# Conformer taps queued behind gate, low half and cast, and spread over the pointwise units

## The chip, the cores and the metric

The kernel runs on one core of one Trainium2 chip. The metric is the device time of one execution in microseconds (us). The engines are TensorE (PE; its weight loads are PEld), VectorE (DVE), ScalarE (ACT), GpSimd (POOL) and SyncE (SP); SP, ACT and POOL also issue DMAs. Each engine takes its instructions in the order of its own queue.

## The reference

A trunk of two layers over 512 positions and 1024 channels, in float32, with one final RMSNorm. The first layer mixes tokens with a gated DeltaNet, the second with the Conformer's convolution module; each then has cross-attention into 256 memory rows and a squared-ReLU MLP. The change is in the second layer's convolution module:

```python
def conformer_conv(h, w_pw1, b_pw1, w_dw, b_dw, ln_g, ln_b, w_pw2, b_pw2):
    u = h @ w_pw1 + b_pw1
    u = u[..., :D_MODEL] * jax.nn.sigmoid(u[..., D_MODEL:])
    c = causal_depthwise_conv(u, w_dw) + b_dw          # 31 taps per channel
    c = jax.nn.silu(layer_norm(c, ln_g, ln_b))
    return c @ w_pw2 + b_pw2
```

## The kernel before

Weights are kept at float32's accuracy by splitting: a half of a weight tile (128 rows, 1024 columns, 512 KB) is loaded by SP into `raw`, ScalarE casts it to the matmul type (`wh`, the high half, line 259), and VectorE or POOL subtracts that from the raw value (`wl`, the low half, line 73). TensorE then does three matmuls for each 128 columns: high by high, high by the low half of the activations, low by high. Three `wh`/`wl` pairs are held (`NW`), so a cast can write only when TensorE is done with the pair three units back. `wsplit` makes these pairs; `POOL_LO` lists the units whose low half POOL makes (7, 8, 10 to 16, 18 and 20 of the Conformer layer), all others are VectorE's.

The Conformer layer runs the units of `CONV_SEQ`: 16 pointwise units (24 matmuls each, two units to one of eight channel tiles `m`, in the order `MORD` = 0, 1, 4, 2, 5, 3, 6, 7), then 16 units of the next cross-attention's keys and values, which are there to keep TensorE busy. "Unit 13" below is the fourteenth of these 32. After each second pointwise unit `pw_ev` makes the gate of a channel tile: two products on VectorE (`sg`, `pa`), a sigmoid on ScalarE, and the gate itself on VectorE (line 79, writing `pa` or `gl`).

The 31-tap convolution is done in three ways. Tiles 4 to 7: the gate `gl` is stored to DRAM by ScalarE's queue, read back in another order into `xg` by SP's queue (`spill`, `fill`), and convolved by matmuls (`conv`, tile `cv`), after which VectorE adds the bias (`cyp`). Tiles 1, 2 and 3: one VectorE instruction for each tap (line 1547, "a tap", accumulating in PSUM in `ca`). Tile 0: a product on ScalarE (`cvp`, line 1530) and an addition on POOL (line 73) for each tap. The last five taps of tile 3 are also products and POOL's additions (`cb`), joined by one VectorE addition. When a tile's last tap is done, ScalarE copies the result out of `ca` (lines 1534, 1550, 1568), and four transposes (`cvT`, `turn`) bring it to rows of positions. LayerNorm's statistics are VectorE's (`bn`, line 1618); their sums over groups go through two tiny matmuls (`ln`, line 1654) whose operand is `lw`.

`TAPS_U` says how many taps of VectorE are put into the program after each unit, and `taps_pool(2)` puts two products and additions after each. A scheduler then orders each engine's queue; it may let an instruction pass earlier ones that are not ready by its own reckoning. `tc.issue_after(x)` keeps what is traced inside it behind `x` on `x`'s engine. Before the change only units from 16 on hold VectorE's taps back in this way (the list `gate`, from the unit before); `wsplit` also holds some casts and low halves back.

Of the kernel before, what the change touches and what calls it, by code (L numbers as in the profile page):

```python
# [11 lines left out]
ALU = mybir.AluOpType  # L12
# [26 lines left out]
def tile_trunk(ctx, tc, xT, memT, x_d, mem_d, prm_d, adt_d, bdw_d, tap_d, fin_d, first_d, w_ab, w_kq, w_v, w_z, w_dno, w_pw1, w_pw2,  # L39
# [14 lines left out]
    def nm(s):  # L54
        cnt[0] += 1
        return f"{s}_{cnt[0]}"

    def slot(dt=F32, s="u", shape=(P, NT)):
        return up.tile(list(shape), dt, tag="u", name=nm(s))
# [12 lines left out]
    def tt(e, o, a, b, op):  # L72
        r = e.tensor_tensor(out=o, in0=a, in1=b, op=op)  # L73
        if e is pool:
            last_pool[:] = [r]
        return r

    def stt(o, a, s, b, op0, op1):
        return dve.scalar_tensor_tensor(out=o, in0=a, scalar=s, in1=b, op0=op0, op1=op1)  # L79
# [17 lines left out]
    def pc(name, i=0):  # L97
        return (gn0 if name == "dn_norm" else prm)[:, OFF[name] + i:OFF[name] + i + 1]
# [128 lines left out]
    ws = {"next": 0, "split": 0, "load": 1, "raw": {0: raw0}, "hl": {}}  # L227
# [4 lines left out]
    def wload():  # L232
        u = ws["load"]
        ws["load"] += 1
        src = loads[u]
        raw = fsp.tile([P, 1024], F32, tag="fs", name=nm("t")) if u in sums7 else raw_tile()
        nc.sync.dma_start(out=raw, in_=src[0])
        for a in src[1:]:
            more(raw, a)
        ws["raw"][u] = raw  # L240
# [5 lines left out]
    def wsplit():  # L246
        u = ws["split"]
        ws["split"] += 1
        while ws["load"] <= need[u]:
            wload()  # L250
        (kind, i, *j), hf = order[u]
        raw = combos7(i, j[0], hf) if kind == "dn7" else ws["raw"].pop(need[u])
        h = wp.tile([P, 1024], F32R, tag="wh", name=nm("wh"), bufs=NW)
        lo = wp.tile([P, 1024], F32R, tag="wl", name=nm("wl"), bufs=NW)
        first = behind.get((kind, 0, 0) if kind == "pw2" else (kind, i, hf))
        if first is None and u in (3, 4):
            first = [ws["rb"]]
        with tc.issue_after(first[0].ins) if first else behind_merge():
            ins = [act.copy(h, raw)]  # L259
        if u < 3:  # L260
            tc.keep_in_program_order(ins[0])
        gp = u - conv0 in POOL_LO
        low = first[1] if first and len(first) > 1 else ws.get("tap")
        with tc.issue_after(low.ins) if low else nullcontext():
            ins.append(tt(pool if gp else dve, lo, raw, h.bitcast(F32), ALU.subtract))
        if not gp:
            ws["ins"] = ins[1]
        if u < 3:
            tc.keep_in_program_order(ins[1])
        ws["hl"][u] = (h, lo)  # L270
        if kind == "dn7":
            after7(i, j[0], hf)

    def wnext(key, hf):
        i = ws["next"]
        assert order[i] == (key, hf), (order[i], key, hf)
        while ws["load"] <= need[min(i + NRAW + 1 + 2 * (order[i][0][0] in ("up", "dn7")), len(order) - 1)]:
            wload()
        ready = NW - (order[i] == (("do", 1), 1) or i in (conv0 - 1, conv0)) if i > 2 else (1, 2, 1)[i]
        while ws["split"] < min(i + ready, len(order)):  # L280
            wsplit()
        ws["next"] += 1
        return ws["hl"].pop(i)
# [3 lines left out]
    def behind_merge():  # L287
        return tc.issue_after(ahead[0].ins) if ahead else nullcontext()
# [3 lines left out]
    def combos7(layer, g, u):  # L292
        name, h = order7(layer, g)[u // 2][1], u % 2
        if name == "T4" or name == "T2" and g < 3:
            return T7[h]
        t = ws["raw"].pop(need[u + base7[layer, g]])
        if name == ("T2" if g == 3 else "T1"):
            T7[h] = t
        return t

    def after7(layer, g, u):
        name, h = order7(layer, g)[u // 2][1], u % 2
        if name == "T2" or name == "T1" and g < 3:
            more(T7[h], block(layer, g, "22" if name == "T1" else "21", h))
# [119 lines left out]
    def root_table():  # L424
        tc.keep_in_program_order(act.activation(small(1), eps_ln, AF.Sqrt))
# [666 lines left out]
    def phased(t):  # L1092
        return t.rearrange("p (t s) -> p s t", s=PH)

    def by_phase(t):
        return t.rearrange("p (s t) -> p s t", s=PH)
# [368 lines left out]
    def conformer(norm, hres, nxt, rest):  # L1465
        xs = norm.xs
        st, x16 = {}, {}
# [8 lines left out]
        def pw_mm(i, hf):  # L1476
            m = MORD[i]
            w, st[m, hf] = wnext(("pw1", i), hf), psum("pw")
            if i:
                return proj(w, xs, st[m, hf], inside={STAT: lambda: (norm.stat(), pw_ev(0))} if (i, hf) == (1, 0) else None)  # L1480
            proj(w, xs, st[m, hf], 0, 4)
            if hf == 0:
                st["w"] = w
                return rest()
            proj(st.pop("w"), xs, st[0, 0], 4, 8)
            proj(w, xs, st[0, 1], 4, 8)

        def pw_ev(m):
            sg = slot(s="sg")
            tt(dve, sg, st.pop((m, 1)), norm.rb, ALU.mult)  # L1490
            act.activation(sg, sg, AF.Sigmoid, bias=pc("b_pw1", 8 + m))
            a = slot(s="pa")
            pa = tt(dve, a, st.pop((m, 0)), norm.rb, ALU.mult)
            if m < NTAP:
                x = wp.tile([P, 544], F32, tag="cv", name=nm("xn"), bufs=NCV)[:, 0:542]
                pool.memset(x[:, 0:30], 0.0)
                stt(a, a, pc("b_pw1", m), sg, ALU.add, ALU.mult)
                act.copy(phased(x[:, 30:542]), by_phase(a))
                (todo if m else todo_p).extend((dve_conv if m else pool_conv)(m, x))
                return  # L1500
            gl, x = [t.rearrange("p (j t) -> p j t", t=34) for t in (
                fsp.tile([P, 1024], F32, tag="fs", name=nm("gl"))[:, 0:544],
                wp.tile([P, 544], F32, tag="cv", name=nm("xg"), bufs=NCV))]
            with tc.issue_after(pa.ins):
                dve.memset(gl[:, :, 0:2], 0.0)
            stt(gl[:, :, 2:34], by_phase(a), pc("b_pw1", m), by_phase(sg), ALU.add, ALU.mult)
            x16[m] = x, gl, drp.tile([P, PH, 34], F32, tag="gd", name=nm("gd"))

        def spill(m):
# [8 lines left out]
        todo, todo_p, acc = [], [], {}  # L1518
# [52 lines left out]
            return [lambda d=d: tap(d) for d in range(n)] + [join]  # L1571

        def taps_pool(n):
            for _ in range(min(len(todo_p), n)):
                todo_p.pop(0)()

        def taps_dve(n):
            for _ in range(min(len(todo), n)):
                todo.pop(0)()
# [118 lines left out]
        gate, stack = [], ExitStack()  # L1698
        for i, (kind, u) in enumerate(CONV_SEQ):
            if kind == "p":  # L1700
                pw_mm(*divmod(u, 2))
                if u % 2 and u > 1:
                    pw_ev(MORD[u // 2])
            else:
                kv_unit(1, u, (LN_SUM[i], lnw.pop("sum")) if i in LN_SUM else None)

            for ins in gate:
                stack.enter_context(tc.issue_after(ins.ins))
            taps_dve(TAPS_U[i])
            stack.close()  # L1710
            taps_pool(2)
            for what, m, *more_ in after.pop(i, ()):
                {"t": taps, "c": conv, "l": ln, "s": lambda m: root_table(), "o": ln_out, "d": turn,
                 "m": moments, "w": spill, "r": fill}[what](m, *more_)
                if what == "c":
                    for ins in gate:
                        stack.enter_context(tc.issue_after(ins.ins))
                    taps_dve(TAPS_C[m])
                    stack.close()
                taps_pool(1 if what == "c" else 0)  # L1720
            gate = [x for x in (ws["ins"], mem.get("kf")) if x is not None] if i >= 15 else []
# [45 lines left out]
    nc.sync.dma_start(out=prm, in_=prm_d)  # L1767
    nc.sync.dma_start(out=adt, in_=adt_d.partition_broadcast(P))
    wsplit()
    for c in range(4):  # L1770
        if c == 3:
# [77 lines left out]
    for gq in range(2):  # L1849
# [12 lines left out]
        a, b = (4 * gq, 4 * gq + 1), (4 * gq + 2, 4 * gq + 3)  # L1862
# [7 lines left out]
        n = 0  # L1870
# [59 lines left out]
    h, rest = mlp7(0, n2, h, n3, lambda: (mem_gain(1, 0), taps(NTAP, *range(9)), selections()))  # L1930
    n4 = Norm("xa_norm1")
    h = conformer(n3, h, n4, rest)
    n5 = Norm("mlp_norm1")
    h = xattn(1, n4, h, n5)
# [45 lines left out]
TAPQ = {0: 12, 4: 44}  # L1980
TAPV = (37, 38, 39, 40, 69, 69, 70, 71)
STAT = 3
TAPS_U = (4,) * 7 + (6,) * 9 + (3,) * 8 + (0,) * 8
TAPS_C = {4: 0, 5: 0, 6: 0, 7: 0}
SHARE = 5
POOL_LO = (7, 8, 10, 11, 12, 13, 14, 15, 16, 18, 20)
# [113 lines left out]
```

## Time and profile before

| | |
|---|---|
| median of 3 runs | 1440.28 us (1439.27 to 1440.81) |
| the profiled execution | 1439.24 us, its span 1437.5 us |
| TensorE busy | 1426.3 us (99% of the span), granted clock 0.999 |
| VectorE, ScalarE, POOL busy | 1053.9, 760.8, 242.6 us |
| the Conformer layer | pointwise units about 787 to 887 us, keys and values to about 942 us of the span |
| in 785 to 890 us | TensorE 102.4, VectorE 93.6, ScalarE 60.6, POOL 66.2 of 105 us |

Busy time of TensorE is modelled, since its matmuls are pipelined: a step from one matmul of 512 columns to the next is 0.23 us, and the row shows 0.39. What counts is its idle time. Rows of a timeline give the start in us, the duration, the engine, the line, what is written and read, and in brackets how long the engine was idle before it and what ended that.

### The profile page before, as it was taken

What the parts mean: (1) busy time and instruction counts of PE and PEld (TensorE: products, weight loads), DVE (VectorE), ACT (ScalarE), POOL (GpSimd) and SP (SyncE); (2) the same over time, 40 slices, a digit from 0 to 9 for tenths busy, and PEclk for the clock granted to TensorE, in tenths of its full rate; (3) what the DMA queues carried; (4) which work ended last, traced back from release to release, by engine and by line L of the source; (5) the groups of instructions that cost most, each with busy time, mean ns of one, the idle gap of its engine ahead of it and who ended that gap; (6) DMA issues with size and microseconds to landing.
All of it is one profiled execution on the core that took longest, in us unless ns stands there. A gap on an engine that the chain in (4) does not pass through costs nothing.

```text
span 1437.5 us, 20460 instructions
## 1 busy us (share of the span) xinstructions
PE 1426.3 (99%) x7786; PEld 1191.4 (83%) x7786; DVE 1053.9 (73%) x1629; ACT 760.8 (53%) x1279; POOL 242.6 (17%) x244
## 2 busy tenths in 40 slices
PE   9999999999999999999999999999999999999998
PEld 7887888888888888888888878888888888888886
DVE  6989999877555766767679799985555766767677
ACT  6757856655444454434355655564444644444354
POOL 1302200102113010010000378111112010010100
PEclk9999999999999999999999999999999999999999
DMA  8232225522214576575766448742215476675853
GB/s 301 72 117 75 70 92 162 190 86 92 74 46 128 150 177 175 143 204 132 195 166 208 154 131 250 261 151 92 74 52 139 119 184 167 148 213 136 219 148 89
DMA packets 71859, 207.83 MB, mean 145 GB/s; under 512 B 15440, under 2 KB 16592, under 8 KB 71760
## 3 DMA queue, kind: packets, MB, share of 16 engines
q1 hardware_dynamic: 60960, 169.22, 36.1%
q0 software_dynamic: 9792, 35.66, 14.3%
q10 hardware_dynamic: 1008, 1.64, 0.3%
q8 instruction: 61, 1.00, 0.3%
q14 instruction: 38, 0.31, 0.1%
HBM read 203.28 MB, written 3.21 MB: 144 GB/s over the span
## 4 chain that ended last, share of the span: by engine, by line
PE 94%; DVE 3%; ACT 1%; issue 1%; POOL 1%; DMA 0%; SPq 0%; DVEq 0%; POOLq 0%; ACTq 0%
PE up L319 8%; PE up L320 8%; PE up L321 8%; PE dn L1263 7%; PE dn L1264 7%; PE dn L1265 7%; PE h L319 3%; PE h L320 3%; PE h L321 3%; PE xo L320 2%; PE q L320 2%; PE q L321 2%; PE xo L319 2%; PE xo L321 2%; PE q L319 2%; PE pw L319 2%
## 5 line engine op out<-in xcount | busy, mean ns | idle before, releaser
L259 ACT CAST wh<-raw 128x1024 fp32r<-128x1024 f32 x259 | 271.0, 1050 | 326.3 <-issue 98.1
L73 DVE TENSOR_TENSOR wl<-raw,wh 128x1024 fp32r<-128x1024 f32 (+1 forms) x251 | 307.8, 1228 | 92.0 <-ACT wh L259 89.9
L319 PE MATMUL up<-xh,wh 128*128 128x512 f32 x512 | 199.6, 390 | 0.0
L321 PE MATMUL up<-xh,wl 128*128 128x512 f32 x512 | 199.5, 390 | 0.0
L320 PE MATMUL up<-xl,wh 128*128 128x512 f32 x512 | 199.4, 390 | 0.0
L319 PEld LDWEIGHTS up<-xh,wh 128*128 128x128 f32 x512 | 96.1, 188 | 20.1
L321 PEld LDWEIGHTS up<-xh,wl 128*128 128x128 f32 x512 | 96.1, 188 | 19.9
L320 PEld LDWEIGHTS up<-xl,wh 128*128 128x128 f32 x512 | 96.2, 188 | 19.9
L244 POOL DMA_DIRECT2D t<-w_dn x48 | 42.1, 915 | 378.1 <-DVE wl L73 271.9
L1263 PE MATMUL dn<-wh,ah 128*128 128x512 f32 (+1 forms) x260 | 100.7, 387 | 0.0
L1265 PE MATMUL dn<-wl,ah 128*128 128x512 f32 (+1 forms) x260 | 100.6, 387 | 0.0
L1264 PE MATMUL dn<-wh,al 128*128 128x512 f32 (+1 forms) x260 | 100.5, 387 | 0.0
L79 DVE SCALAR_TENSOR_TENSOR rl<-up,rb 128x512 f32<-128x512 f32 x64 | 44.2, 690 | 58.7 <-PE up L321 58.7
L259 ACT CAST wh<-t 128x1024 fp32r<-128x1024 f32 x44 | 46.4, 1054 | 57.3 <-PE dn L1264 42.4
L73 DVE TENSOR_TENSOR wl<-t,wh 128x1024 fp32r<-128x1024 f32 x44 | 53.8, 1224 | 30.2 <-ACT wh L259 30.1
L73 POOL TENSOR_TENSOR sq<-sq,sq 128x512 f32<-128x512 f32 x26 | 42.8, 1648 | 168.4 <-ACT sq L447 151.3
L1547 DVE SCALAR_TENSOR_TENSOR ca<-xn,prm,ca 128x512 f32<-128x512 f32 x85 | 64.0, 753 | 5.2 <-ACT ca L1544 2.9
L73 DVE TENSOR_TENSOR acc<-acc,dn 128x512 f32<-128x512 f32 x99 | 66.6, 682 | 1.0
L319 PE MATMUL h<-xh,wh 128*128 128x512 f32 x160 | 63.9, 399 | 0.0
L321 PE MATMUL h<-xh,wl 128*128 128x512 f32 x160 | 62.5, 391 | 0.0
L320 PE MATMUL h<-xl,wh 128*128 128x512 f32 x160 | 62.4, 390 | 0.0
L73 DVE TENSOR_TENSOR al<-u,ah 128x512 fp32r<-128x512 f32 x64 | 44.1, 689 | 21.3 <-ACT ah L380 21.3
(427 smaller groups left out, 3491.4 us busy)
## 6 DMA issues: line engine op xcount, KB each, us to landing
raw<-w_dn SPq DMA_DIRECT2D x68, 512.0 KB, 4.5
raw<-w_up SPq DMA_DIRECT2D x64, 512.0 KB, 4.9
t<-w_dn POOLq DMA_DIRECT2D x48, 512.0 KB, 6.6
tap<-tap SPq DMA_DIRECT2D x48, 256.0 KB, 6.0
raw<-w_pw SPq DMA_DIRECT2D x24, 512.0 KB, 4.1
raw<-w_dn POOLq DMA_DIRECT2D x20, 512.0 KB, 6.4
raw<-w_k SPq DMA_DIRECT2D x16, 512.0 KB, 3.8
raw<-w_vv SPq DMA_DIRECT2D x16, 512.0 KB, 5.8
```

Of the source, the lines that this page charges most:

```text
L73: r = e.tensor_tensor(out=o, in0=a, in1=b, op=op)
L79: return dve.scalar_tensor_tensor(out=o, in0=a, scalar=s, in1=b, op0=op0, op1=op1)
L244: nc.gpsimd.dma_start(out=t, in_=a, accum_op=ALU.add)
L259: ins = [act.copy(h, raw)]
L319: pe.matmul(ps, wh, xh, start=first, stop=False)
L320: pe.matmul(ps, wh, xl, start=False, stop=False)
L321: pe.matmul(ps, wl, xh, start=False, stop=last)
L1263: pe.matmul(ps, xh, w[0][:, s], start=opens and k == 0, stop=False, skip_group_check=True)
L1264: pe.matmul(ps, xl, w[0][:, s], start=False, stop=False, skip_group_check=True)
L1265: pe.matmul(ps, xh, w[1][:, s], start=False, stop=k == 3, skip_group_check=True)
L1547: first["tap"] = dve.scalar_tensor_tensor(out=a, in0=src, scalar=w, in1=a, op0=ALU.mult, op1=ALU.add)
```

## The change

It does three things. The taps of VectorE after pointwise units 4 to 15 are held behind the latest gate (`st["ev"]`) and the latest low half that VectorE made (`ws["ins"]`). Each unit's additions of POOL, with ScalarE's products, are held behind the latest cast (`ws["wh"]`, on ScalarE) and the latest low half that POOL made (`ws["lo"]`, on POOL). And units 3 to 6 put 5 taps into the program instead of 4, units 7 and 8 put 5 instead of 6.

```diff
@@ wsplit
-        if not gp:
-            ws["ins"] = ins[1]
+        ws["wh"] = ins[0]
+        ws["lo" if gp else "ins"] = ins[1]
@@ pw_ev
-                stt(a, a, pc("b_pw1", m), sg, ALU.add, ALU.mult)
+                st["ev"] = stt(a, a, pc("b_pw1", m), sg, ALU.add, ALU.mult)
...
-            stt(gl[:, :, 2:34], by_phase(a), pc("b_pw1", m), by_phase(sg), ALU.add, ALU.mult)
+            st["ev"] = stt(gl[:, :, 2:34], by_phase(a), pc("b_pw1", m), by_phase(sg), ALU.add, ALU.mult)
@@ taps_pool
-            for _ in range(min(len(todo_p), n)):
-                todo_p.pop(0)()
+            with tc.issue_after(ws["wh"].ins), tc.issue_after(ws["lo"].ins) if "lo" in ws else nullcontext():
+                for _ in range(min(len(todo_p), n)):
+                    todo_p.pop(0)()
@@ conformer, the loop over CONV_SEQ
+            if kind == "p" and u > 3:
+                gate = [st["ev"], ws["ins"]]
             for ins in gate:
                 stack.enter_context(tc.issue_after(ins.ins))
             taps_dve(TAPS_U[i])
@@
-TAPS_U = (4,) * 7 + (6,) * 9 + (3,) * 8 + (0,) * 8
+TAPS_U = (4,) * 3 + (5,) * 6 + (6,) * 7 + (3,) * 8 + (0,) * 8
```

What the scheduler makes of it is seen in the engines' queues. First VectorE's, from the gate of tile 1 (`pa_7823`) on, before; `gl` is tile 4's gate, and the `wl` is the low half of unit 9:

```order
L79 SCALAR_TENSOR_TENSOR pa_7823<-pa_7823,prm,sg_7820 128x512
L1547 SCALAR_TENSOR_TENSOR ca_7829<-xn_7825,prm,ca_7829 128x512 x15
L73 TENSOR_TENSOR sg_7924<-pw_7899,rb_7755 128x512
L73 TENSOR_TENSOR pa_7927<-pw_7852,rb_7755 128x512
L1505 MEMSET gl_7929 128x16x2
L1547 SCALAR_TENSOR_TENSOR ca_7829<-xn_7825,prm,ca_7829 128x512
L79 SCALAR_TENSOR_TENSOR gl_7929<-pa_7927,prm,sg_7924 128x16x32
L1547 SCALAR_TENSOR_TENSOR ca_7829<-xn_7825,prm,ca_7829 128x512 x4
L73 TENSOR_TENSOR wl_7989<-raw_7893,wh_7988 128x1024
```

Twenty taps stand ahead of unit 9's low half, 15 of them ahead of tile 4's first product. The same place of VectorE's queue after the change:

```order
L79 SCALAR_TENSOR_TENSOR pa_7823<-pa_7823,prm,sg_7820 128x512
L1547 SCALAR_TENSOR_TENSOR ca_7829<-xn_7825,prm,ca_7829 128x512 x9
L73 TENSOR_TENSOR sg_7926<-pw_7901,rb_7755 128x512
L73 TENSOR_TENSOR pa_7929<-pw_7853,rb_7755 128x512
L1505 MEMSET gl_7931 128x16x2
L79 SCALAR_TENSOR_TENSOR gl_7931<-pa_7929,prm,sg_7926 128x16x32
L1547 SCALAR_TENSOR_TENSOR ca_7829<-xn_7825,prm,ca_7829 128x512 x5
L73 TENSOR_TENSOR wl_7993<-raw_7895,wh_7992 128x1024
```

Six taps moved from ahead of the two products to behind the gate and the low half, and no tap is left between the products and the gate.

The second place is where tile 2's taps end. VectorE's queue after the change, from unit 17's low half to unit 19's (`ca_8128` is tile 2):

```order
L73 TENSOR_TENSOR wl_8549<-raw_8371,wh_8548 128x1024
L1547 SCALAR_TENSOR_TENSOR ca_8128<-xn_8026,prm,ca_8128 128x512
L73 TENSOR_TENSOR cyp_7582<-cv_8424,bdw_7584 128x8x32
L1547 SCALAR_TENSOR_TENSOR ca_8128<-xn_8026,prm,ca_8128 128x512
L73 TENSOR_TENSOR cyp_7583<-cv_8424,bdw_7584 128x8x32
L1547 SCALAR_TENSOR_TENSOR ca_8128<-xn_8026,prm,ca_8128 128x512 x2
L73 TENSOR_TENSOR wl_8655<-raw_8546,wh_8654 128x1024
L73 TENSOR_TENSOR sg_8577<-pw_8552,rb_7755 128x512
```

Before, tile 2's last tap stood ahead of tile 6's products, 6 taps of tile 3 ahead of unit 17's low half; now four of tile 2's taps stand behind that low half, and unit 19's follows the last of them at once. ScalarE's queue there, before (`ca_8491` is the copy of tile 2's result; the casts are those of units 17, 18 and 19):

```order
L1550 COPY ca_8491<-ca_8128 128x512
L1530 ACTIVATE cvp_8496<-xn_7762,prm 128x512
L1530 ACTIVATE cvp_8499<-xn_7762,prm 128x512
L1530 ACTIVATE cvp_8529<-xn_7762,prm 128x512
L259 CAST wh_8546<-raw_8369 128x1024
L259 CAST wh_8607<-raw_8456 128x1024
L1530 ACTIVATE cvp_8591<-xn_7762,prm 128x512
L1491 ACTIVATE sg_8575<-sg_8575,prm 128x512
```

and after the change:

```order
L259 CAST wh_8548<-raw_8371 128x1024
L1550 COPY ca_8491<-ca_8128 128x512
L1530 ACTIVATE cvp_8498<-xn_7762,prm 128x512
L1530 ACTIVATE cvp_8501<-xn_7762,prm 128x512
L1530 ACTIVATE cvp_8531<-xn_7762,prm 128x512
L259 CAST wh_8609<-raw_8458 128x1024
L259 CAST wh_8654<-raw_8546 128x1024
L1530 ACTIVATE cvp_8593<-xn_7762,prm 128x512
L1491 ACTIVATE sg_8577<-sg_8577,prm 128x512
```

Unit 17's cast moved ahead of the copy, and unit 19's joined unit 18's, behind the copy and three products.

The third place is TensorE's queue at the first sum of LayerNorm's statistics, among the matmuls of the values (`V`), before:

```order
L371 MATMUL V_9047<-wh_9084,mh_7305 128x512
L372 MATMUL V_9047<-wl_9085,mh_7305 128x512
L373 MATMUL V_9047<-wh_9084,ml_7306 128x512
L1654 MATMUL ln_9119<-lw_9118,sel_7209 128x16
L371 MATMUL V_9047<-wh_9084,mh_7305 128x512
```

and after the change:

```order
L372 MATMUL V_9048<-wl_9085,mh_7305 128x512
L373 MATMUL V_9048<-wh_9084,ml_7306 128x512
L1655 MATMUL ln_9119<-lw_9118,sel_7209 128x16
L371 MATMUL V_9160<-wh_9102,mh_7178 128x512
L372 MATMUL V_9160<-wl_9103,mh_7178 128x512
```

The sum moved 9 matmuls later, from the middle of unit 27 to its end; tile 3's transposes moved 20 matmuls later. The rest of TensorE's queue is the same. VectorE's queue now has two more instructions ahead of the sum's operand, the low half of unit 29 (`wl_9126`) and one of the values (`Vl_9143`).

## The prediction

> **What bounds the kernel now.** I read the page's first part, then who TensorE waited for, then busy time by stage, then the timelines of VectorE, ScalarE, POOL and TensorE side by side over the Conformer layer.
>
> ```profile
> span 1437.5 us, 20460 instructions
> PE 1426.3 (99%) x7786; PEld 1191.4 (83%) x7786; DVE 1053.9 (73%) x1629; ACT 760.8 (53%) x1279; POOL 242.6 (17%) x244
> PE pw L321 <- DVE wl L73: 2.1, 1, 2.1
> PE pw L321 <- POOL wl L73: 0.5, 1, 0.5
> 785.00:890.00 105.00, 102.44 (x652) 83.12 (x651) 93.61 (x133) 60.62 (x86) 66.18 (x43) 1.00 0.52 159
> 890.00:940.00 50.00, 50.00 (x479) 44.57 (x478) 46.85 (x96) 30.15 (x49) 12.19 (x7) 1.00 0.79 260
> ```
>
> TensorE (first busy column of the two stretches) is busy 99% of the span: only its idle time can be won, and a late operand costs its whole lateness. In the Conformer layer it waits twice, for a low half of weights made by VectorE and for one made by POOL, 2.6 us in all. That is the ceiling of the gain, 0.18%. But VectorE (third column) is busy 94% from 890 to 940: there both engines are full, and whatever VectorE loses earlier lands on TensorE. The two waits, in rows of the timelines (start, duration, engine, what, and in brackets the idle time before it with what ended it):
>
> ```profile
> 821.56 11.84 DVE L1547 SCALAR_TENSOR_TENSOR ca<-xn,prm,ca 128x512 f32<-128x512 f32 x15 [1.98 <-ACT ca L1544]
> 833.31 0.69 DVE L73 TENSOR_TENSOR sg<-pw,rb 128x512 f32<-128x512 f32 x1
> 834.03 0.72 ACT L1491 ACTIVATE sg<-sg,prm 128x512 f32<-128x512 f32 x1 [8.73 <-DVE sg L73]
> 835.18 0.75 DVE L79 SCALAR_TENSOR_TENSOR gl<-pa,prm,sg 128x512 f32<-128x512 f32 x1
> 835.84 3.12 DVE L1547 SCALAR_TENSOR_TENSOR ca<-xn,prm,ca 128x512 f32<-128x512 f32 x4
> 836.50 1.99 ACT L259 CAST wh<-raw 128x1024 fp32r<-128x1024 f32 x2
> 838.48 0.39 PE L320 MATMUL pw<-xl,wh 128*128 128x512 f32 x1
> 838.87 2.00 DVE L73 TENSOR_TENSOR wl<-raw,wh 128x1024 fp32r<-128x1024 f32 x1
> 840.93 0.50 PE L321 MATMUL pw<-xh,wl 128*128 128x512 f32 x1 [2.06 <-DVE wl L73]
> 867.43 0.50 PE L321 MATMUL pw<-xh,wl 128*128 128x512 f32 x1 [0.50 <-POOL wl L73]
> ```
>
> Fifteen taps stand ahead of the gate's first product (sg). ScalarE's sigmoid waits 8.73 us for it, the cast behind the sigmoid is late, and unit 9's low half starts at 838.87, 0.16 us after unit 9 wants it (838.48 plus one matmul step of 0.23). A tap costs 0.79 us (11.84/15).
>
> **The exclusion that prices the rest.** Low halves, gates and POOL's additions all read two operands from SBUF.
>
> ```profile
> 829.66 1.29 POOL L73 TENSOR_TENSOR ca<-ca,cvp 128x512 f32<-128x512 f32 x1
> 835.51 4.29 POOL L73 TENSOR_TENSOR ca<-ca,cvp 128x512 f32<-128x512 f32 x3 [4.56 <-ACT cvp L1530]
> 839.81 3.34 POOL L73 TENSOR_TENSOR wl<-raw,wh 128x1024 fp32r<-128x1024 f32 x1
> 875.52 4.76 POOL L73 TENSOR_TENSOR wl<-raw,wh 128x1024 fp32r<-128x1024 f32 x2
> 877.99 0.68 DVE L73 TENSOR_TENSOR sg<-pw,rb 128x512 f32<-128x512 f32 x1
> 879.47 1.38 DVE L79 SCALAR_TENSOR_TENSOR gl<-pa,prm,sg 128x512 f32<-128x512 f32 x1 [0.15 <-ACT sg L1491]
> 902.22 3.53 POOL L73 TENSOR_TENSOR cb<-cb,cvp 128x512 f32<-128x512 f32 x2
> 902.38 2.21 DVE L73 TENSOR_TENSOR wl<-raw,wh 128x1024 fp32r<-128x1024 f32 x1
> ```
>
> A VectorE operation that meets a running POOL operation ends about 0.55 us (gate) or 1.1 us (low half) after POOL's: POOL's pair of low halves ends at 880.28, the gate at 880.85 instead of 880.22. A POOL operation that meets VectorE's waits likewise (3.34 instead of 2.4). Taps read PSUM and never stretch. So one of VectorE's gates costs up to 1.3 us against an addition and up to 2.4 us against a low half. A gate with no tap to fill its sigmoid's time starts 1.48 us after its first product (877.99, 879.47).
>
> **The change, step by step.** Table and gates belong together: they move the taps and remove no instruction. Times below are the start of a stretch plus its durations, with TensorE 2.06 us earlier than before from unit 9 on.
>
> *First wait.* Now 9 taps, then the gate, 5 taps, the low half. First product at 828.54 (821.56 plus 9 taps), gate ready at 830.0, held by the addition that runs to 830.95, ended at 831.5; five taps; the low half at 835.3 to 836.6. Unit 9 wants it at 838.7. The 2.06 us go, with 2.1 us to spare.
>
> *Second wait.* POOL's order is unchanged up to the low half of unit 20. But ScalarE's products for POOL (cvp) now stand behind a store that waits for the next gate and a copy that waits for channel tile 1's last tap.
>
> ```profile
> 856.60 8.43 POOL L73 TENSOR_TENSOR ca<-ca,cvp 128x512 f32<-128x512 f32 x6 [0.76 <-ACT cvp L1530]
> 864.99 4.75 POOL L73 TENSOR_TENSOR wl<-raw,wh 128x1024 fp32r<-128x1024 f32 x2
> ```
>
> After 836.6: 4 taps, first product, tap, second product, gate, 10 taps: next first product at 849.8, gate ready at 851.3, held by a POOL low half to 852.8, last tap of tile 1 done at 853.5. ScalarE's copy and product then let POOL start its six additions at 854.75; unit 13's low half follows at 863.0 to 865.3. TensorE wants it at 866.93 less 2.06, at 864.9: the 0.5 us stay.
>
> *The gates behind.* Third gate: 7 taps, two bias additions, 3 taps after 853.5 put its first product at 861.7 and it is ready at 863.2, while POOL is in that low half: ended 865.9 (1.9 lost). Eleven taps, first product 874.4, gate ready 876.4, POOL in the second of its next two low halves until 878.25: ended 878.8 (1.75 lost). This is the choice with least margin: had VectorE come 0.3 us earlier to the third gate, POOL would have waited instead.
>
> *The new wait.* After that gate come 7 taps, unit 17's low half (1.2), 4 taps and 2 bias additions: channel tile 2's last tap ends at 888.85. VectorE's next instruction is unit 19's low half. Its cast stands on ScalarE behind the copy of that same last tap, three products and another cast:
>
> ```profile
> 881.27 0.57 ACT L1550 COPY ca<-ca 128x512 f32<-128x512 f32 x1
> 881.75 1.94 ACT L1530 ACTIVATE cvp<-xn,prm 128x512 f32<-128x512 f32 x3
> 883.60 1.04 ACT L259 CAST wh<-raw 128x1024 fp32r<-128x1024 f32 x1
> 896.15 1.23 DVE L73 TENSOR_TENSOR wl<-raw,wh 128x1024 fp32r<-128x1024 f32 x1 [1.21 <-ACT wh L259]
> 894.88 0.28 PE L321 MATMUL K<-mh,wl 128*128 128x256 f32 x1
> 926.62 0.17 DVE L73 TENSOR_TENSOR lw<-lw 128x16 f32<-128x16 f32 x1
> 926.85 0.40 PE L1654 MATMUL ln<-lw,sel 128*128 128x16 f32 x2
> ```
>
> Copy 0.5, products 1.85, casts 0.95 and 1.04, hand-over 0.1: VectorE stands still 4.4 us, to 893.2, where before it lost 1.21 at this low half. POOL's last of three additions runs until 894.2, so the low half ends at 895.25 and POOL's own for unit 18, queued behind, at 897.5. TensorE wants that one at 894.88 less 2.06, at 892.8: a wait of 4.7 us.
>
> *Stores and fills.* The change moves the gates of tiles 4 to 7, and with each the store on ScalarE's queue and the fill on SP's that bring it back reordered.
>
> ```profile
> DMA to landing us min/median/max: 2.1/5.9/7.2
> DMA to landing us min/median/max: 3.4/4.6/5.9
> 916.72 3.19 DVE L1618 BATCH_NORM_STATS2 bn<-cyp 128x6 f32<-128x128 f32 x16
> 922.67 2.47 DVE L1618 BATCH_NORM_STATS2 bn<-cy 128x6 f32<-128x512 f32 x4
> ```
>
> The first row is the stores', the second the fills'. Tile 5's fill passes three tap loads on SP's queue and its gate ends 4 us earlier: nothing to pay. Tile 7's gate ends at 898.1, its store leaves near 901 behind a copy that waits for POOL, and its matmuls come near 912: 11 us for two transfers of at most 13.1. A wait of up to 2 us there would lie inside the one that follows. On POOL, unit 20's low half now passes the four shared additions: it comes earlier, and nothing waits for it.
>
> *What settles the end.* Then: gate of tile 7 (held, 898.1), 7 taps to 903.4, a K low half that waits for ScalarE and POOL until 905.45, and unit 21's low half at 909.3. From there to the operand of the first LayerNorm sum (lw) stand 12 taps (8.3 us with steps of 0.67 to 0.79), 8 weight low halves (9.0, 1.13 from start to start), four of K and V (2.4), 20 statistics (5.5 by the two rows above), two bias additions, the joining addition and three small ones (2.0): 27.2 us, so the operand is there at 936.5. Before it was there at 926.8 and TensorE took it at 926.85 without idling. In the new TensorE order the sum stands 9 matmuls later (2.04 us), so before's clock for that place is 928.9 and the changed kernel is at 936.65: +7.75 us. TensorE's earlier waits are inside this one and don't add. Behind it the chain to the second sum takes 3.9 us, TensorE's 18 matmuls 4.1: no further wait, and nothing is given back.
>
> **The sum.** The profiled execution took 1439.24 us (span 1437.5 and 1.7 around it); the median of the runs is 1.0 higher. +7.75 gives 1447.0. If the third gate wins its race, POOL's low half slips instead (unit 13 waits 1.4), VectorE is 1.9 earlier, and the same working gives +5.9. With 0.3 us between the two I take the middle, 1446.0.
>
> [...] The granted clock stays at 1.00 in the stretch with the 2.06 us wait, so the sum above lets TensorE resume at full speed after 4.7 and 4.2 us as well. [...]
>
> **The rivals.**
> 1. *POOL and VectorE happen not to meet.* Without a held gate or low half, tile 2's last tap ends at 884.6, the 4.4 us stand-still remains, and the operand comes at 931.7: +2.8, 1442.0. For it: before lost only 2.4 us that way in the layer (0.78, 0.63, 0.99). Against: POOL is busy 66 of 105 us in the first stretch.
> 2. *The gain stays.* It decides whether tile 2's last tap ends by 884.1; then the copy, a product, three additions and a low half (8.7 us) reach unit 18 in time, and if the 27 us behind also find slack, 2.06 to 2.56 us are won: 1436.7. Against: VectorE's 94% from 890 to 940.
> [...]
> 4. *The change does nothing.* Excluded: VectorE's order differs at every gate.
>
> **Chances.** Held gates, +4 to +9: 0.55. Rival 1, up to +4: 0.25, most of it within the bound. Rival 2: 0.10. Rival 3: 0.06. Something else late, such as tile 7's fill before its matmuls: 0.04. The likeliest gives 1446.0. Range 1438.5 to 1450.5: it leaves out rival 2 and the tail. What a measurement here can tell from no change is about 0.2%, 2.9 us: faster by more 0.09, within 0.29, slower 0.62.
>
> **What the next profile would show.** Right: no wait of TensorE near 838; VectorE idle some 4 us before a low half near 889, ended by a cast; TensorE waiting near 893 for POOL's low half and longest at the LayerNorm sum near 932, for lw. Stretched gates wherever POOL is in a low half. [...]

## The result and the profile after

| | before | after |
|---|---|---|
| median | 1440.29 us (1439.27 to 1440.81) | 1450.00 us (1449.46 to 1451.23) |
| ratio | | 1.0070, 95% interval 1.0052 to 1.0087 |
| profiled execution, its span | 1439.24, 1437.5 us | 1449.46, 1447.8 us |

The change makes the kernel slower by 9.7 us. The page's first lines, the waits of TensorE and the same two stretches as before (busy time of TensorE, its loads, VectorE, ScalarE and POOL, then the granted clock, DMA share and GB/s):

```profile
span 1447.8 us, 20470 instructions
PE 1430.0 (99%) x7786; PEld 1193.9 (82%) x7786; DVE 1056.7 (73%) x1629; ACT 761.3 (53%) x1279; POOL 242.6 (17%) x244
PE K L321 <- POOL wl L73: 3.8, 1, 3.8
PE ln L1655 <- DVE lw L73: 3.6, 1, 3.6
PE pw L321 <- POOL wl L73: 0.8, 1, 0.8
785.00:890.00 105.00, 104.16 (x662) 84.92 (x661) 94.13 (x131) 58.35 (x83) 61.13 (x39) 1.00 0.54 164
890.00:940.00 50.00, 42.59 (x428) 38.21 (x427) 43.56 (x75) 28.13 (x47) 16.39 (x10) 0.96 0.72 234
```

The wait of 2.06 us for unit 9's low half is gone. In its place stand a wait of 3.8 us in the K units and one of 3.6 us at the first LayerNorm sum, both in the stretch from 890 to 940 where TensorE did not idle before. VectorE, which was full there with 46.85 us, is busy for only 43.56, and the mean clock is 0.96.

VectorE's timeline from tile 1's first tap to the operand of the sum, in extract:

```profile
823.43 7.09 DVE L1547 SCALAR_TENSOR_TENSOR ca<-xn,prm,ca 128x512 f32<-128x512 f32 x9 [1.99 <-ACT ca L1544]
831.90 1.49 DVE L79 SCALAR_TENSOR_TENSOR gl<-pa,prm,sg 128x512 f32<-128x512 f32 x1 [0.15 <-ACT sg L1491]
837.13 1.24 DVE L73 TENSOR_TENSOR wl<-raw,wh 128x1024 fp32r<-128x1024 f32 x1
853.28 1.35 DVE L79 SCALAR_TENSOR_TENSOR gl<-pa,prm,sg 128x512 f32<-128x512 f32 x1 [0.15 <-ACT sg L1491]
864.86 2.88 DVE L79 SCALAR_TENSOR_TENSOR pa<-pa,prm,sg 128x512 f32<-128x512 f32 x1 [0.19 <-ACT sg L1491]
878.28 2.37 DVE L79 SCALAR_TENSOR_TENSOR gl<-pa,prm,sg 128x512 f32<-128x512 f32 x1
888.30 1.53 DVE L1547 SCALAR_TENSOR_TENSOR ca<-xn,prm,ca 128x512 f32<-128x512 f32 x2
894.27 2.10 DVE L73 TENSOR_TENSOR wl<-raw,wh 128x1024 fp32r<-128x1024 f32 x1 [4.43 <-ACT wh L259]
897.76 1.37 DVE L79 SCALAR_TENSOR_TENSOR gl<-pa,prm,sg 128x512 f32<-128x512 f32 x1 [0.15 <-ACT sg L1491]
...
937.27 0.16 DVE L73 TENSOR_TENSOR lw<-lw 128x16 f32<-128x16 f32 x1
```

Five of the six gates (line 79) take 1.35 to 2.88 us, where before five took 0.75 to 0.82 and one 1.38, and unit 19's low half comes after 4.43 us in which VectorE does nothing. What ScalarE did then, and POOL's chain to unit 13's and unit 18's low halves:

```profile
889.92 0.59 ACT L1550 COPY ca<-ca 128x512 f32<-128x512 f32 x1 [7.74 <-DVE ca L1547]
890.41 1.95 ACT L1530 ACTIVATE cvp<-xn,prm 128x512 f32<-128x512 f32 x3
892.26 1.98 ACT L259 CAST wh<-raw 128x1024 fp32r<-128x1024 f32 x2
```

```profile
856.69 8.17 POOL L73 TENSOR_TENSOR ca<-ca,cvp 128x512 f32<-128x512 f32 x6 [2.60 <-ACT cvp L1530]
864.82 5.20 POOL L73 TENSOR_TENSOR wl<-raw,wh 128x1024 fp32r<-128x1024 f32 x2
...
891.27 4.02 POOL L73 TENSOR_TENSOR ca<-ca,cvp 128x512 f32<-128x512 f32 x3 [6.73 <-ACT cvp L1530]
895.25 3.33 POOL L73 TENSOR_TENSOR wl<-raw,wh 128x1024 fp32r<-128x1024 f32 x1
```

Both engines had waited for tile 2's last tap: ScalarE 7.74 us for the tap, and POOL 6.73 us for the products behind the copy. TensorE at the two waits, and behind the second:

```profile
898.63 0.58 PE L321 MATMUL K<-mh,wl 128*128 128x256 f32 x1 [3.81 <-POOL wl L73]
...
937.48 0.40 PE L1655 MATMUL ln<-lw,sel 128*128 128x16 f32 x2 [3.60 <-DVE lw L73]
...
938.97 0.57 PE L373 MATMUL V<-wh,ml 128*128 128x512 f32 x1
939.33 0.63 PE L371 MATMUL V<-wh,mh 128*128 128x512 f32 x1
939.76 0.63 PE L372 MATMUL V<-wl,mh 128*128 128x512 f32 x1
...
942.61 0.39 PE L373 MATMUL V<-wh,ml 128*128 128x512 f32 x1
```

From 938.97 to 942.61 nine steps take 3.64 us, 0.40 each on average where the normal step is 0.23: 1.6 us more. The granted clock was 0.50 from 939.03 to 942.44 us, as the section on the hardware shows.

**Where the 10.2 us between the two profiled executions are.** Tile 1's first tap starts 1.87 us later than before (823.43 against 821.56), behind code that is the same in both kernels. In the eight kernels below, which share that code (but for two gates in experiment 3), it starts between 821.93 and 824.00, and before's start is the earliest of the ten; it is taken here as spread from one execution to the next. The sum comes at 937.48 instead of 928.9 (before's clock for its new place), which is 8.6, and 6.7 without the start. The half clock adds 1.6. The rest of the kernel is equal within 0.1 us. For the runs below a last column therefore gives the profiled execution's time less its late start: 1439.2 before, 1447.6 after.

**What VectorE's chain is made of.** From tile 1's first tap to the operand (start of the one to the end of the other) it took 105.23 us before and takes 114.00 now, 8.77 more. Summed over the rows of the two timelines, with overlaps counted once: gates 4.7 and 10.2 us (+5.5), idle time between the rows 2.4 and 6.8 (+4.4), one low half of V more (+0.7), one more low half of weights but less time held in them (+0.5). Against these stand 2.0 us from taps, more of which now alternate with other instructions, and 0.3 from the rest.

### The profile page after: what moved, and what is told of

It reads as the page before. It is cut to its first block, busy times and chain, and to the rows that moved or that the text cites. A ratio compares the mean times of both kernels' runs of the same rounds, so it can differ in the third digit from the quotient of the medians.

```text
span 1447.8 us, 20470 instructions
## 1 busy us (share of the span) xinstructions
PE 1430.0 (99%) x7786; PEld 1193.9 (82%) x7786; DVE 1056.7 (73%) x1629; ACT 761.3 (53%) x1279; POOL 242.6 (17%) x244
## 4 chain that ended last, share of the span: by engine, by line
PE 83%; DVE 11%; DMA 2%; issue 2%; ACT 2%; POOL 1%; SPq 0%; ACTq 0%; DVEq 0%; POOLq 0%
PE up L319 8%; PE up L320 8%; PE up L321 8%; PE dn L1263 7%; PE dn L1264 7%; PE dn L1265 7%; DVE ca L1547 2%; PE xo L320 2%; PE q L319 2%; PE q L320 2%; PE xo L321 2%; PE xo L319 2%; PE q L321 2%; DVE wl L73 2%; PE pw L319 1%
```

## The experiments

| kernel | tile 1's first tap | VectorE's chain | median | ratio, 95% | profiled, less late start |
|---|---|---|---|---|---|
| before | 821.56 | 105.23 | 1440.29 | | 1439.2 |
| after | 823.43 | 114.00 | 1450.00 | 1.0052 to 1.0087 | 1447.6 |
| 1 table alone | 823.00 | 105.55 | 1440.99 | 0.9992 to 1.0011 | 1440.0 |
| 2 gates, old table | 822.77 | 116.15 | 1451.72 | 1.0067 to 1.0097 | 1450.1 |
| 3 gate's operand in PSUM | 822.12 | 113.14 | 1448.37 | 1.0035 to 1.0068 | 1447.9 |
| 4 late copy | 822.20 | 109.94 | 1444.58 | 1.0021 to 1.0040 | 1444.3 |
| 5 POOL relieves VectorE | 824.00 | 112.92 | 1444.74 | 1.0021 to 1.0047 | 1445.2 |
| 6 gates at units 4, 5 | 822.53 | 104.96 | 1441.25 | 0.9998 to 1.0017 | 1439.0 |
| 7 the same, POOL relieves | 821.93 | 103.47 | 1438.46 | 0.9976 to 0.9994 | 1437.8 |
| 8 wait split in two | 823.17 | 114.17 | 1447.42 | 1.0034 to 1.0061 | 1446.2 |

The intervals are against the kernel before in the same session (median 1440.26 for 1 to 4, 1440.51 for 5 to 8).

My theory: VectorE is one chain up to the sum, and what it loses (gates held by POOL, the stand-still behind tile 2's copy) lands on the end. Rivals: the new table does it, the gates are long for another reason, POOL's chain is late by itself, and the clock falls for some other cause than the wait.

**1. The table alone**

```diff
-TAPS_U = (4,) * 7 + (6,) * 9 + (3,) * 8 + (0,) * 8
+TAPS_U = (4,) * 3 + (5,) * 6 + (6,) * 7 + (3,) * 8 + (0,) * 8
```

> The kernel before with the new table of taps alone: no gate on VectorE's taps, none on POOL's additions. Its queues differ from the kernel before's only behind tile 7's gate (a few taps of tile 3 and one K low half change places), and TensorE's order is the same. Theory (VectorE's lost time between its gates makes the loss, and that comes from the order, not from the table): the two waits of 2.06 and 0.5 us stay, time 1440.3 within 1.0 us. Rival (the table carries the loss, since more taps stand late): 1446 to 1450 us, with a wait at the LayerNorm sum.

Waits of TensorE in this run:

```profile
PE pw L321 <- DVE wl L73: 2.0, 1, 2.0
PE pw L321 <- POOL wl L73: 0.6, 1, 0.6
PE ln L1654 <- DVE lw L73: 0.2, 1, 0.2
```

The old waits are there, and the time is before's. The table alone does nothing.

**2. The gates with the old table.** The table stays as before; `taps_pool` as before too.

> The changed kernel with the old table of taps: VectorE's taps held behind the gate and the low half as in the changed kernel. (With or without the third part, POOL's additions held behind the cast, all queues come out the same, so this run leaves that part out.) The LayerNorm sum stands later in TensorE's order here as in the changed kernel. Theory: the order behind the gates alone makes the loss: gates of VectorE held by POOL (sum of their time beyond 0.75 us above 4 us), a stand-still of about 4 us before unit 19's low half, a wait of over 3 us at the LayerNorm sum: 1447 to 1451 us. Rival (gates and table are both needed, since only with the even table do tile 2's taps end behind unit 17's low half): 1439 to 1442 us.

```profile
PE ln L1654 <- DVE lw L73: 6.4, 1, 6.4
PE cv L1599 <- DMA xg<-gd: 3.4, 1, 3.4
PE cvT L1586 <- ACT ca L1568: 2.0, 1, 2.0
```

```profile
891.03 1.71 DVE L73 TENSOR_TENSOR wl<-raw,wh 128x1024 fp32r<-128x1024 f32 x1 [3.44 <-ACT wh L259]
```

The gates alone carry the loss, 0.7 us beyond the upper end I gave. Two of these three waits were not in my list: a fill's transfer and tile 3's copy were late as well. The stand-still is there (3.44 us, the second view, VectorE's timeline). With gates, the new table is worth 1.7 us between the medians; without them nothing. The third part of the change, POOL's additions held behind cast and low half, leaves the order of every queue as it is without it, so it has no share.

**3. The gate reads PSUM**

```diff
-            a = slot(s="pa")
-            pa = tt(dve, a, st.pop((m, 0)), norm.rb, ALU.mult)
+            a = st.pop((m, 0))
+            pa = tt(dve, a, a, norm.rb, ALU.mult)
```

> The changed kernel, but the product that the gate reads (pa) is left in the PSUM tile it came from, so that the gate reads one operand of PSUM and one of SBUF instead of two of SBUF; TensorE's and POOL's queues are the same as in the changed kernel. Theory (a VectorE operation with two SBUF operands waits for a running POOL operation): all gates take 0.75 to 0.85 us, also where POOL runs; the five long gates of the changed kernel (1.49, 1.35, 2.88, 2.37, 1.37) give back 5.7 us, the stand-still before unit 19's low half stays at 3.5 to 5 us, the operand of the LayerNorm sum comes about 5.5 us earlier and TensorE waits there under 1.5 us, without the stretch at half clock behind it: 1443 to 1446 us. Rival (the gates are long for another reason, such as their strided writes or POOL's memory traffic): gates stay as they are, 1449 to 1451 us.

VectorE's rows at unit 9's low half, at the third gate and at unit 19's low half, with POOL's two low halves at the third gate:

```profile
836.17 3.29 DVE L73 TENSOR_TENSOR wl<-raw,wh 128x1024 fp32r<-128x1024 f32 x1
...
864.38 4.75 POOL L73 TENSOR_TENSOR wl<-raw,wh 128x1024 fp32r<-128x1024 f32 x2
864.91 0.75 DVE L79 SCALAR_TENSOR_TENSOR pa<-pw,prm,sg 128x512 f32<-128x512 f32 x1 [0.79 <-ACT sg L1491]
...
891.36 2.13 DVE L73 TENSOR_TENSOR wl<-raw,wh 128x1024 fp32r<-128x1024 f32 x1 [3.75 <-ACT wh L259]
```

The mechanism is shown: each of the six gates takes 0.75 us, the third one too, inside a POOL low half as in the changed kernel, where it took 2.88. But the time was missed, 1448.4 where I said 1443 to 1446. The twelve low halves ahead of the sum, which still read two SBUF operands, take 18.6 us together instead of 14.8 (unit 9's 3.29), and idle time rises from 6.8 to 8.7, with three waits of 0.79 for the sigmoid and one of 2.17 that were not there. Freeing one kind of instruction passed the meeting with POOL on to the next. The sum was waited for 4.27 us, and half clock behind it lasted twice as long (0.50 from 934.50 to 941.32 us, 6.8 us instead of 3.4).

**4. Tile 2's copy behind the casts**

```diff
@@ dve_conv, last tap
+                    if m == 2:
+                        st["late"] = st.pop("ca")
+                        return
                     act.copy(by_phase(acc[m]), phased(st.pop("ca")))
@@ turn
+            if m == 2:
+                with tc.issue_after(ws["wh"].ins):
+                    act.copy(by_phase(acc[m]), phased(st.pop("late")))
```

> The changed kernel, but ScalarE's copy of tile 2's result is put behind the latest cast before tile 2's transposes, instead of directly behind the last tap; unit 19's low half then stands behind tile 7's gate on VectorE. Tile 2's transposes stand later in TensorE's order. The held gates stay. Theory (copy, three products and two casts stand between tile 2's last tap and unit 19's low half and cost 4.4 us): VectorE's idle time there falls below 1.2 us, TensorE's wait for unit 18's low half falls below 1 us, the wait at the sum from 3.6 us to below 1 us, no half clock behind it: 1443.5 to 1446 us. Rival (POOL and ScalarE are late there for their own queues' work and the copy is only the last of it): the stand-still or the wait for unit 18 keeps over 3 us, 1447 to 1450 us.

TensorE's waits, and VectorE's row of the sum's operand:

```profile
PE cvT L1593 <- ACT ca L1590: 4.0, 1, 4.0
PE cv L1606 <- DMA xg<-gd: 0.9, 1, 0.9
931.96 0.18 DVE L73 TENSOR_TENSOR lw<-lw 128x16 f32<-128x16 f32 x1
```

The stand-still is gone, and VectorE's chain is 4.06 us shorter. Idle time gives 3.2 of it. Another 2.0 come from two low halves, one of weights and one of V, that no longer stand ahead of the operand: the scheduler has put the sum back to the place in TensorE's order that it had before the change, where TensorE wants it 2.04 us earlier. Gates (0.5), taps (0.4) and small ones (0.3) take more. Against before's clock for its place the sum is thus 4.7 us late instead of 6.7, so 2.0 us of the stand-still came off the end. With the wait at the sum the half clock behind it went too: the mean clock of 0.93 from 890 to 940 us has room for the 6.8 us at half named below and no more. The waits for unit 18's low half and at the sum are gone, and the time is within what I said. A wait of 4.0 us for the late copy itself took their place at the transposes, with half clock for 6.8 us behind it (steps of 0.21 us between the matmuls of 256 columns up to 904.16, of 0.12 from 904.33 on). TensorE then reaches the sum at 932.19, 0.05 us after its operand, so that VectorE's chain alone would give the same end. The chain is still 4.7 us longer than before's, which is the held gates (10.7 us against 4.7) and 1.2 of idle time, less 1.0 from low halves that are held for less time and 1.5 from the taps.

**5. POOL makes two more low halves** (`POOL_LO` with 22 and 24).

> The changed kernel, with POOL making two more low halves, those of units 22 and 24, which VectorE made between tile 7's gate and the LayerNorm sum; the sum keeps its place in TensorE's order. Theory (from tile 1's first tap to the sum's operand VectorE is one chain, and every us of it lands on the end): two low halves of 1.13 us less, operand 2.3 us earlier, wait at the sum 1.3 instead of 3.6 us and no half clock behind it (1.7 us): 1445 to 1447.5 us. Rival (POOL's two low halves of 2.4 us hold VectorE's other low halves as much as they relieve it, as in the run with the gate's operand in PSUM): 1448.5 to 1451 us.

```profile
936.75 0.17 DVE L73 TENSOR_TENSOR lw<-lw 128x16 f32<-128x16 f32 x1
936.98 0.40 PE L1655 MATMUL ln<-lw,sel 128*128 128x16 f32 x2 [0.60 <-DVE lw L73]
942.10 0.39 PE L373 MATMUL V<-wh,ml 128*128 128x512 f32 x1
```

The wait at the sum falls to 0.6 us, and the clock behind it is 1.00 (939.00 to 942.40 us). The chain, however, shrinks by 1.1 us instead of the 2.3 that I counted: the low halves' time falls by 2.3, but idle time and taps take 1.0 more. The rest of the shorter wait is TensorE's, which reached the sum at 936.38 instead of 933.88: 0.6 of these 2.5 us come from unit 18's low half, which ended at 899.16 instead of 898.58, and 0.4 from a wait at the values. The other 1.5 are by my estimate a second step of 3.41 us at half clock behind unit 18's wait. The time, 1444.7, lies just under my range. The profiled execution took 1447.6, 2.9 us above the median; 2.44 of that are its late start, and less that start it gives 1445.2.

**6. Gates after units 4 and 5 alone**

```diff
-            if kind == "p" and u > 3:
+            if kind == "p" and 3 < u <= 5:
                 gate = [st["ev"], ws["ins"]]
```

The old table stands, and `taps_pool` is as before.

> The kernel before with VectorE's taps held behind the gate and the low half after units 4 and 5 alone (table as before). TensorE's order is the one of before, unit 9's low half stands where it stands in the changed kernel, and tile 2's last tap is far ahead of unit 19's low half, so that its copy holds nobody up. The first wait (2.06 us) goes in any case. Theory: then the time changes by what VectorE's chain to the LayerNorm sum gains or loses, but by no more than 2.06 us downwards: without a stand-still, with some gates held by POOL (0 to 4 us more than before): 1439 to 1444 us. Rival (the first wait was the bound and its end is kept): 1437.5 to 1438.5 us.

```profile
PE ln L1654 <- DVE lw L73: 2.2, 1, 2.2
PE K L321 <- POOL wl L73: 0.6, 1, 0.6
```

This is the change's own aim without most of its damage: the waits of 2.06 and 0.5 us at the pointwise units are gone. Held gates still take 6.6 us instead of 4.7 and idle time is 4.2 instead of 2.4, but low halves and taps give 3.8 back, so VectorE's chain is as long as before's (104.96 against 105.23), and the 2.06 us come back as a wait of 2.2 us at the sum. Nothing is won, because TensorE and VectorE reached the sum together before (926.85 and 926.79).

**7. The same, and POOL makes the low halves of units 22 and 24**

> The run with gates after units 4 and 5 alone, and POOL making the low halves of units 22 and 24 besides. TensorE's order is the one of before. Theory (VectorE's chain sets the end): 2.3 us less than that run, down to the floor of 2.06 us under the kernel before: 1437.5 to 1442 us. Rival (POOL's low halves hold VectorE's as much as they relieve it): the same as that run within 0.5 us.

```profile
span 1436.4 us, 20466 instructions
PE ln L1654 <- DVE lw L73: 0.7, 1, 0.7
```

The chain falls by 1.5 us, the wait at the sum from 2.2 to 0.7, and the time to 1438.46 us, 0.9985 of the kernel before's in the same session (1440.51; interval 0.9976 to 0.9994). This version beats both kernels, the one before by 2.1 us.

**8. The wait at the sum split in two**

```diff
-                lnw["sum"] = lambda: pe.matmul(ps[:, 16 * step:16 * step + 16], same_t, e16, start=True, stop=True)
+                def total():
+                    for _ in range(0 if step else 6):
+                        pe.matmul(ps[0:20, 256:384], m20, ident, start=True, stop=True)
+                    lnw["at"] = pe.matmul(ps[:, 16 * step:16 * step + 16], same_t, e16, start=True, stop=True)
+
+                lnw["sum"] = total
@@ the loop over CONV_SEQ
-                kv_unit(1, u, (LN_SUM[i], lnw.pop("sum")) if i in LN_SUM else None)
+                with tc.issue_after(lnw["at"].ins) if i == 28 else nullcontext():
+                    kv_unit(1, u, (LN_SUM[i], lnw.pop("sum")) if i in LN_SUM else None)
```

> The changed kernel with six small matmuls (128 columns, float32) into unused columns of the LayerNorm sum's PSUM tile, directly ahead of the sum, from an operand that VectorE has ready 1.9 us before the sum's own; the matmuls behind are held behind the sum as before. They split TensorE's wait of 3.6 us in two, each under 2 us, and end no later than the sum's operand is there. Theory (the half clock behind the wait comes from the wait's length): the sum starts as late as before, but no matmul behind it runs at half clock: steps of 0.23 us, 1.7 us less, 1447.5 to 1449 us. Rival (the clock falls for another reason): a stretch of 3.4 us at 0.50 behind the sum again, 1449.5 to 1451 us.

TensorE's timeline, and busy time in the 3.41 us that were at half clock after the change:

```profile
935.50 1.49 PE L1657 MATMUL ln<-ident,lw 128*20 128x128 f32 x12 [1.66 <-DVE lw L73]
937.40 0.40 PE L1658 MATMUL ln<-lw,sel 128*128 128x16 f32 x2 [0.41 <-DVE lw L73]
942.28 0.40 PE L372 MATMUL V<-wl,mh 128*128 128x512 f32 x1
939.13:942.54 3.41, 3.41 (x18) 2.85 (x17) 2.26 (x10) 1.33 (x2) 0.00 (x0) 1.00 0.74 243
```

The sum starts as late as in the changed kernel (937.40), but the clock behind it is 1.00, and the time is 1447.4 us, 0.1 under the range I gave (1447.8 in the profiled execution, 1446.2 less its late start). Filling the wait with useless work gives 1.4 us by that column, and 2.6 between the medians, which also hold the spread of the starts.

## Why the prediction was right, point by point

Times of after are given less its late start of 1.87 us. The way and the path were right: held gates, the stand-still and VectorE's chain to the sum. The clock was left out, and that the sum's lateness came out as forecast is luck, as shown below.

- **First wait**: the 2.06 us go. Unit 9's low half was put at 835.3 to 836.6 and ran from 835.3 to 836.5.
- **Second wait**: it stays, 0.8 us where 0.5 was said. POOL's additions start at 854.82 (854.75 said) and unit 13's low half at 862.95 (863.0).
- **Held gates**: ends of 831.5, 852.8, 865.9 and 878.8 were said; 831.5, 852.8, 865.9 and 878.8 came out. The race at the third gate went the way I thought likelier. Experiment 3 shows what the holding rests on: inside a POOL low half the third gate took 2.88 us with two operands in SBUF and 0.75 with one of them in PSUM.
- **The stand-still**: 4.4 us said, 4.43 measured. Unit 18's wait was said to be 4.7 and is 3.8. The term that was too big lies ahead of the stand-still: from the fourth gate's end to tile 2's last tap 10.05 us were said and 9.2 measured. The first seven taps there took 4.6 us, 0.66 a step, where a tap was priced at 0.79. So unit 19's low half, held for as long as said, ended at 894.5 and not at 895.25.
- **What settles the end**: the operand was put at 936.5 and came at 935.6. The sum is thus 6.7 us late, where I had 7.75 in this branch and took 6.8 as the middle of two. The chain was 1.3 us early at unit 21's low half (end 908.0, said 909.3), 0.75 of it from unit 19's, and the rest behind it took 27.6 us where I had counted 27.2. So the 6.8 was met by luck: my working of the branch that came true was 1.05 us too big, and the middle that I took between two branches had 0.95 off. After the sum nothing was given back, as said.
- **The time**: 1446.0 was worked out from before's profiled execution, and the 1.0 us by which the median lies above it was named but not added; with it the forecast of the median would have been 1447.1. From 1446.0 to 1450.00 it is 4.0 us: 1.6 of the clock, 1.87 of the late start, and 0.5 by which the median after lies above its profiled execution. The upper end of the range, 1450.5, is only 0.5 us above the median.
- **Stores and fills**: no wait for a transfer in the layer, as said. Experiment 2 has one of 3.4 us.
- **Rival 3** (the clock falls behind the two waits): this is the step that failed. I gave it 0.06 and argued from the 1.00 beside a wait of 2.06 us. The granted clock fell to 0.50 behind both waits (898.07 to 901.48 and 939.03 to 942.44 us), and behind the second a step took 0.43 us (939.33 to 939.76) instead of 0.23. I also mispriced it, with 4.4 us: that was an estimate with the clock at half for as long as each wait lasted, which no run shows. It was at half for one step of 3.41 us behind each (two behind one wait in experiments 3 and 4), and the first of these lies inside the later wait for VectorE. It adds 1.6 us. Without it the late-start column would read 1446.0, the predicted time.
- **Rival 1** (no meetings, 1442): experiment 3 took the gates' meetings away and won 1.6 us between the medians and nothing less the late starts, since the meetings pass on to the low halves. The rival's own case, no meeting at all, no run shows, so its price stays untested.
- **Rival 2** (the gain stays): in experiment 6 tile 2's copy delays no low half of VectorE, unit 18's comes within 0.6 us, and the gain still does not stay. The 27 us behind have no slack, as the argument against it said.

Of the 9.7 us between the medians, 6.7 and 1.6 are accounted for. The remaining 1.4 us I could not place: it is of the size of the spread of the starts. The clock may hold part of it, which is not shown: the three executions that were not profiled have mean clocks of 0.994 to 0.995, the profiled one 0.996, and by an estimate from 3.41 us at half in 1448 us one further step at half clock lowers that mean by 0.0012.

## What to carry to other kernels

Where two engines reach a meeting point together, removing a wait of one of them wins nothing until the other's chain is shortened as well; look at which engine makes the next operand, and how much slack it has, before reordering. When held-back work moves a producer's last instruction directly ahead of a consumer on the same engine, follow what the other engines do between them: here copy, products and casts of ScalarE stood in between, and VectorE stood still for 4.4 us. And an operation that contended with another engine did not stop contending here when its victim was changed: in experiment 3 the gates fell to 0.75 us each, and the twelve low halves rose from 14.8 to 18.6 us together. Count the meetings over the whole stretch.

## What the runs showed of the hardware

**The clock fell after a stretch that was only about half idle.** In the changed kernel's trace the changes of the granted clock around the two waits lie on a grid of 3.413 us: the half clock ran from 898.07 to 901.48 and from 939.03 to 942.44 us, and 901.48 to 939.03 is 11.0 such steps. Cut on this grid, the changed kernel reads:

```profile
894.66:898.07 3.41, 0.16 (x2) 0.00 (x0) 3.26 (x5) 1.27 (x3) 3.41 (x2) 1.00 0.32 120
898.07:901.48 3.41, 2.85 (x13) 2.85 (x14) 3.30 (x5) 1.77 (x3) 3.41 (x3) 0.50 0.52 120
...
932.20:935.61 3.41, 1.69 (x8) 1.07 (x6) 3.41 (x7) 2.94 (x6) 0.00 (x0) 1.00 0.00 0
935.62:939.03 3.41, 1.55 (x8) 1.33 (x9) 3.31 (x7) 0.55 (x2) 0.00 (x0) 1.00 0.59 189
939.03:942.44 3.41, 3.41 (x10) 2.67 (x9) 1.70 (x9) 0.26 (x1) 0.00 (x0) 0.50 0.75 256
```

After the window with TensorE busy for 1.69 us the clock was 1.00 in the next one; after the one with 1.55 us it was 0.50. In experiment 2 a window with 1.57 us was followed by 1.00, so 1.55 and 1.57 of 3.41 us are the closest pair that came out differently here, as far as the modelled ends of matmuls can tell. The wait of 3.60 us was cut by the grid into 1.7 and 1.9, and half clock followed the second part. So the length of a wait alone, as experiment 8's theory had it, didn't settle it: in experiment 2 a wait of 2.00 us that lay in one window (928.69 to 932.10 us, busy for 1.41) was followed by half clock (the mean of 0.92 from 890 to 940 us is what half clock from 932.10 on gives), and one of 3.37 us that the grid cut into 1.8 and 1.5 (the windows busy for 1.57 and 1.88) was not. The fallen clock also stayed: in experiment 3 the window after the sum, busy for 2.59 of 3.41 us at 0.50, was followed by another at 0.50; in the changed kernel one busy for 2.85 us was followed by 1.00. The grid was not tied to the program: the half clock of experiment 3 starts at 934.50 us, 10.67 steps behind the 898.07 of the changed kernel.
